# Sending eighteen more transposes of a decoder kernel through DRAM instead of through TensorE

## The chip, the core and the metric

The kernel runs on one core of one Trainium2 chip. The metric is the device time of one launch in microseconds (us), the median of several runs. Five engines work side by side, each through its own list of instructions in order: PE (TensorE: matmuls and the transposes that are made as matmuls; PEld is its weight load), DVE (VectorE), ACT (ScalarE), POOL (GpSimd) and SP (SyncE), which here issues every DMA. An instruction that has to wait holds up everything behind it on its engine.

## What is computed

Two blocks, one behind the other, on x of 256 rows by 1024. Where the change works:

```python
for l in range(2):                                     # first block
    proj = x @ w_in[l]                                 # split into cb,cc,ch,dq,dk,dv,iq,ik,iw,cq,ck,cv
    y = concat(conv(cb,cc,ch), dsa_attention(dq,dk,dv,iq,ik,iw), chunk_band_attention(cq,ck,cv))
    x = layer_norm(ALPHA*x + y @ w_mix_out[l])
    q = x @ w_mq[l]; k, v = split(mem @ w_mkv[l])      # memory cross attention, 4 heads of 256
    x = layer_norm(ALPHA*x + softmax(q k' / 16) v @ w_mo[l])
    x = layer_norm(ALPHA*x + squared_relu(x @ w_ff1[l]) @ w_ff2[l])
for i in range(4):                                     # second block
    mix = retention | dilated attention | gMLP | retention
    # gMLP: s = tril(w_s[g]) @ vn + b_s,  mix = (u * s) @ w_out
    x = x + rmsnorm(mix); x = x + rmsnorm(swiglu(rmsnorm(x))); x = x + gate * (p[i] @ w_proj)
```

Every projection is made in split precision: a 32-bit operand is cut into a high part and the rest, and three matmuls (high x high, high x rest, rest x high) are added.

## The kernel before

The 256 rows are two tiles of 128, each worked by its own generator, "thread 0" and "thread 1". Both use one stream of weight blocks, so a block is loaded and cut once; thread 1 follows thread 0 by a few blocks. A block is 512 KB (384 KB for the groups named cq, ck and cv): `load` issues its DMA on SP into one of 5 raw buffers, `split` has ACT cast the high part `wh` (L284 or L225) and DVE subtract the rest `wl` (L232 or L228); the raw buffer is free again when the rest has been cut, and so DVE sets when SP may issue the load five blocks on.

`proj` (L402) makes one 512-wide projection from four blocks and calls `flush` behind each block; `flush` runs work that was put off to that place: `due` counts down in blocks, `behind` holds the attention heads of a mixer, one step a block. The order of the instructions on each engine is then set by a scheduler, which works with its own estimates of durations; it places the DMA issues in SP's list too.

Matmuls need their left operand transposed. There are two ways to get it:

- `transpose4` (L276): up to four 128x128 matmuls by an identity (L279) into one PSUM bank, then one copy out of the bank by ACT or DVE. The tiles are called cqp, ckp, mTp, mqp and wsp at the five places of this change.
- `trip` (L356) and what calls it: DVE transposes 32x32 blocks into `xt` (L360), four DMAs write it to a DRAM tile `xd` (L364), and one DMA reads it back in turned order (L376, L380 or L386). `turn_to` then copies it in place with ACT (L377), `turn_by_dma` cuts it into high part and rest (L397, L398). The read is put off by BACK = 1 block, the copy by CUT = 3 blocks. `xt` shares two buffers with `ET`, the turned softmax weights of all attention heads, over both threads.

In a mixer (`mixer`, L625) the groups come in the order A, B, cq, ck, cv, F, H, then the memory keys and values (mkv), then the output projection. A and B end in an index score of which DVE takes the 64 largest entries of each row in 8 rounds of MAX8 and MATCH_REPLACE (L689, L690) while PE works on cq and ck. The heads of the first attention (`six_heads` on dqT and dkT: scores `sp`, softmax `ss`, transposes `ptp`, product with the values) run beside cv and F, those of the chunk attention (on cqT and ckT) beside H and mkv. In the first layer the 256 memory rows are transposed too (`memory_rows`, L619), once for both layers.

Of the kernel before, what the change touches and what calls it, by code (L numbers as in the profile page):

```python
# [15 lines left out]
P = 128  # L16
# [14 lines left out]
DEFER = (1, 1, 1, 1, 1, 1, 1, 1)  # L31
# [17 lines left out]
def kernel(  # L49
# [226 lines left out]
    def transpose4(t, srcs, nm, kind="tr"):  # L276
        p = bank(kind, t, [P, 4, P], nm)
        for i, s in enumerate(srcs):
            T.transpose(p[:, i, :], s, ident)  # L279
        return p  # L280
# [26 lines left out]
    def newbank(t):  # L307
        return tuple(sb.tile([P, 4, P], F32R, tag=f"h{t}", name=f"part{t}", bufs=8) for _ in range(2))

    def cut(bank, sl, src, scale=1.0, rows=slice(0, P), hi_eng="s"):  # L310

        hi, lo = bank[0][rows, sl, :], bank[1][rows, sl, :]
        if scale == 1.0:
            copy(hi_eng, hi, src)
            V.tensor_tensor(out=lo, in0=src, in1=hi.bitcast(F32), op=ALU.subtract)
        else:
            S.activation(hi, src, AF.Copy, scale=scale)
            V.scalar_tensor_tensor(out=lo, in0=src, scalar=scale, in1=hi.bitcast(F32), op0=ALU.mult,
                                   op1=ALU.subtract)
# [29 lines left out]
    def defer(t, on, fn):  # L349
        if on:  # L350
            later[t].append(fn)
        else:
            fn()
# [28 lines left out]
    def turn_by_dma(t, src, nkk, parts, j, square=None, at=CUT):  # L382

        back = trip(t, src, nkk)
        z = src
        put_off(t, BACK, lambda: nc.sync.dma_start(z, back))  # L386

        def fin():
            bank = parts.banks[j] = newbank(t)
            zv = z.rearrange("p (i k b) -> p k i b", i=4, k=nkk)  # L390
            hi, lo = (x[:, 0:nkk, :].rearrange("p k (i b) -> p k i b", i=4) for x in bank)
            if square:
                f = sb.tile([P, 4, P], F32, tag=f"tq{t}", name="ffT", bufs=2)
                S.activation(f[:, 0:nkk, :].rearrange("p k (i b) -> p k i b", i=4), zv, AF.Square, scale=square)
                cut(bank, slice(0, nkk), f[:, 0:nkk, :])
            else:
                S.copy(hi, zv)  # L397
                V.tensor_tensor(out=lo, in0=zv, in1=hi.bitcast(F32), op=ALU.subtract)  # L398

        put_off(t, at, fin)  # L400
# [218 lines left out]
    def memory_rows(t):  # L619
        rows = tiles[("memr", t)]  # L620
        m_ = Parts()
        mh = sb.tile([P, 8, P], F32R, tag=f"x{t}", name=f"memHi{t}")
        for b in range(2):
            p = transpose4(t, [rows[:, (4 * b + i) * P:(4 * b + i + 1) * P] for i in range(4)], "mTp")
            m_.banks.append((mh[:, 4 * b:4 * b + 4, :], memLo[:, t, 4 * b:4 * b + 4, :]))  # L625
            cut(m_.banks[b], slice(0, 4), p)
        memT[t] = m_


    def mixer(t, l, xT):  # L630
# [118 lines left out]
        S.copy(cq[:, :384], pq[:, :384])  # L749
        cqT = sb.tile([P, 3, P], F32, tag=f"tq{t}", name="cqT", bufs=2)  # L750

        def turn(src, dst, nm):
            p = transpose4(t, [src[:, i * P:(i + 1) * P] for i in range(3)], nm)
            S.copy(dst, p[:, 0:3, :])

        defer(t, DEFER[6], lambda: turn(cq, cqT, "cqp"))
        if l == 0:
            defer(t, DEFER[6], lambda: memory_rows(t))
        pk = yield from proj(t, xT, ("ck", l), 384)
        ck = sb.tile([P, 512], F32, tag=f"rB{t}", name="ck", bufs=2)  # L760
        S.copy(ck[:, :384], pk[:, :384])
        ckT = get2(("ckT", l), [P, 3, 256], "kv", 4)
        defer(t, DEFER[6], lambda: turn(ck, ckT[:, :, own], "ckp"))

        behind[t].append(six_heads(dqT, lambda h, r: dkT[r:r + 64, :nk], lambda kt, h: shared[("dv", l, kt)],
                                   lambda hs: score.rearrange("p (o k) -> p o k", o=1).to_broadcast([P, len(hs), nk]),
# [73 lines left out]
    def cross(t, l, xT):  # L840
        qT = []
        oT = Parts()
        for j in range(2):
            p = yield from proj(t, xT, ("mq", l, j), 512)
            q = sb.tile([P, 512], F32, tag=f"rA{t}", name="mqr", bufs=2)
            if j:
                V.tensor_scalar(out=q, in0=p, scalar1=0.0625, scalar2=None, op0=ALU.mult)
            else:
                S.mul(q, p, 0.0625)
            pt = transpose4(t, [q[:, i * P:(i + 1) * P] for i in range(4)], "mqp")  # L850
            qT.append(sb.tile([P, 4, P], F32, tag=f"tq{t}", name="mqT", bufs=2))
            copy("s" if j else "v", qT[j], pt)
        for b in range(2):
            kT = shared[("mkT", l, b)]
            sp = bank("at", t, [P, 2, 256], "msp")
            for i in range(2):
                for c in range(2):
                    T.matmul(sp[:, i, :].rearrange("p (i b) -> p i b", b=32), qT[b][:, 2 * i + c, :], kT[:, :, 2 * i + c, :],
                             start=(c == 0), stop=(c == 1))
            pt, et, ev = turn_bank(t, softmax_bank(t, sp, 2, 2), 2)  # L860
            copy("v", et, pt)
            o = pt
            for i in range(2):
                for c in range(2):
                    c0 = 512 * b + 256 * i + 128 * c
                    for kt in range(2):
                        T.matmul(o[:, 2 * i + c, :], shared[("mv", l, kt)][:, c0:c0 + P], ev[:, i, kt, :],
                                 start=(kt == 0), stop=(kt == 1))
            oT.banks.append(newbank(t))
            cut(oT.banks[b], slice(0, 4), o, IALPHA)  # L870
        acc = newacc(t)
        yield from outproj(t, acc, ("mo", l), 8, oT, 0, True, True, xT)
        return acc
# [194 lines left out]
    def gmlp(t, hT, rs):  # L1068
        if t == 0:
            ws = tiles[("gws",)]  # L1070
            G.affine_select(out=ws, in_=ws, pattern=[[0, 8], [-1, P]], compare_op=ALU.is_ge, fill=0.0, base=0,
                            channel_multiplier=1)
            wsT = sb.tile([P, 8, P], F32, tag="kv", name="wsT", bufs=4)
            for b in range(2):
                pt = transpose4(t, [ws[:, 4 * b + k, :] for k in range(4)], "wsp")
                V.tensor_copy(wsT[:, 4 * b:4 * b + 4, :], pt)
            shared["wsT"] = wsT
        wsT = shared["wsT"]
        st_ = small([P, 4, 6], f"gst{t}")
        vs = []  # L1080
        for j in range(4):
            p = yield from proj(t, hT, ("gv", j), 512)
            tag, nb = (f"U{t}", 3) if j < 3 else (EB[0].format(t=t), EB[1])
            v = sb.tile([P, 512], F32, tag=tag, name="gvr", bufs=nb)
            S.activation(v, p, AF.Gelu, scale=rs[:, 0:1])
            V.bn_stats(out=st_[:, j, :], in_=v)
            vs.append(v)
        mv = small([P, 2], f"mv{t}")
        V.bn_aggr(out=mv, in_=st_)
        ve = small([P, 1], f"ve{t}")  # L1090
        V.tensor_scalar(out=ve, in0=mv[:, 1:2], scalar1=EPS, scalar2=None, op0=ALU.add)
        r2 = small([P, 1], f"rs{t}")
        rsqrt(r2, ve)
        gg, gb = tiles[("gmg",)], tiles[("gmb",)]
        for j in range(4):
            sl = slice(512 * j, 512 * j + 512)
            V.tensor_scalar(out=vs[j], in0=vs[j], scalar1=mv[:, 0:1], scalar2=r2[:, 0:1],  # L1097
                            op0=ALU.subtract, op1=ALU.mult)
            V.tensor_tensor(out=vs[j], in0=vs[j], in1=gg[:, sl], op=ALU.mult)  # L1099
            (V if j == 0 else G).tensor_tensor(out=vs[j], in0=vs[j], in1=gb[:, sl], op=ALU.add)  # L1100
        acc = newacc(t)
        oT = Parts()
        for j in range(5):
            if j < 4:
                p = yield from proj(t, hT, ("gu", j), 512)
                u = sb.tile([P, 512], F32, tag=f"rA{t}", name="gur", bufs=2)
                S.activation(u, p, AF.Gelu, scale=rs[:, 0:1])
                sp = bank("tr", t, [P, 2, 256], "gsp")
                o = sb.tile([P, 512], F32, tag=f"rB{t}", name="gor", bufs=2)
                for k in range(2):  # L1110
                    g = 2 * j + k
                    T.matmul(sp[:, k, :], wsT[:, g, :], vs[j][:, 256 * k:256 * k + 256], start=True, stop=True)  # L1112
                for k in range(2):
                    g = 2 * j + k
                    V.scalar_tensor_tensor(out=o[:, 256 * k:256 * k + 256], in0=sp[:, k, :], scalar=gbs[:, g:g + 1],
                                           in1=u[:, 256 * k:256 * k + 256], op0=ALU.add, op1=ALU.mult)
                oT.banks.append(None)
                turn_by_dma(t, o, 4, oT, j)
            if j > 0:
                yield from outproj(t, acc, ("go", j - 1), 4, oT, 4 * j - 4, j == 1, j == 4)  # L1120
        return acc
# [213 lines left out]
```

## Time and profile before

| | |
|---|---|
| median of 3 runs | 2572.3 us (2567.38 to 2573.31) |
| profiled execution | 2566.06 us, its span 2564.3 us, granted TensorE clock 0.999 |
| PE busy | 2521.9 us, 98% of the span |
| DVE / ACT busy | 1823.3 us (71%) / 1501.9 us (59%) |
| DMA engines | 66.4% busy for the queue that SP feeds, 205 GB/s of HBM traffic over the span |

Times in the rows below count from the start of the span. A busy time holds the whole length of each instruction; matmuls are pipelined, so two starts can lie closer together than one of them is long. In brackets at the end of a timeline row stand the idle time of the engine before it and what ended that.

### The profile page before, as it was taken

To read this page: it belongs to the slowest core of one execution; us is meant where nothing else is said; L and a number is where in the kernel's file an instruction comes from. 1 tells how busy PE (TensorE), PEld (TensorE's weight loads), DVE (VectorE), ACT (ScalarE), POOL (GpSimd) and SP (SyncE) were. 2 spreads that over 40 slices of the span, in tenths; PEclk is the share of its full clock that TensorE was granted. 3 is DMA by queue.
4 is the path that set the end of the run, shared out by engine and by line. 5 is a ranking of instruction groups with operands and counts; after the bars stand their busy time and mean duration, and the time that the engine had idled before them with its cause. 6 is when DMAs were issued, how large, how long until landed. Compare 5 with 4: busy or idle time off the path is not lost. (4 is left out here: it accounts for less than half of the span.)

```text
span 2564.3 us, 36170 instructions
## 1 busy us (share of the span) xinstructions
PE 2521.9 (98%) x12100; PEld 2059.6 (80%) x12100; DVE 1823.3 (71%) x3357; ACT 1501.9 (59%) x2856; POOL 60.0 (2%) x88
## 2 busy tenths in 40 slices
PE   8999999999999999999999999999999999999999
PEld 7787787887788778788777787888877887887887
DVE  8865767866766876766866767767767678766666
ACT  6653555654455565555766666557656557565555
POOL 0000000000000000000000000000100000000000
PEclk9999999999999999999999999999999999999999
DMA  6463776554578677677766665777576776766774
GB/s 214 150 215 103 224 245 187 171 192 156 155 233 244 190 235 248 190 240 219 221 204 209 194 208 179 230 214 223 170 257 212 226 221 196 255 220 193 230 208 159
DMA packets 321227, 528.27 MB, mean 206 GB/s; under 512 B 37392, under 2 KB 135824, under 8 KB 319888
## 3 DMA queue, kind: packets, MB, share of 16 engines
q1 hardware_dynamic: 321040, 525.96, 66.4%
q8 instruction: 95, 1.56, 0.3%
q14 instruction: 92, 0.75, 0.1%
HBM read 484.96 MB, written 40.89 MB: 205 GB/s over the span
## 5 line engine op out<-in xcount | busy, mean ns | idle before, releaser
L326 PE MATMUL pj<-wh,part 128*128 128x512 f32 (+3 forms) x4480 | 1415.4, 384 | 4.9 <-ACT part L284 1.4
L326 PEld LDWEIGHTS pj<-wh,part 128*128 128x128 f32 x4480 | 831.2, 188 | 174.3 <-issue 8.9
L326 PE MATMUL pj<-wl,part 128*128 128x512 f32 (+3 forms) x2240 | 852.9, 381 | 1.3 <-DVE wl L228 1.3
L326 PE MATMUL acc<-wh,part 128*128 128x512 f32 x1920 | 582.2, 395 | 12.8 <-ACT part L284 5.9
L326 PEld LDWEIGHTS pj<-wl,part 128*128 128x128 f32 x2240 | 421.9, 188 | 79.1 <-DVE wl L228 2.7
L326 PEld LDWEIGHTS acc<-wh,part 128*128 128x128 f32 x1920 | 356.8, 189 | 92.5 <-ACT part L284 8.4
L326 PE MATMUL acc<-wl,part 128*128 128x512 f32 x960 | 307.1, 393 | 0.1
L232 DVE TENSOR_TENSOR wl<-ff,wh 128x512 fp32r<-128x512 f32 x256 | 169.6, 686 | 102.9 <-ACT wh L284 102.6
L284 ACT CAST wh<-ff 128x512 fp32r<-128x512 f32 x256 | 152.4, 620 | 131.5 <-PE acc L326 64.6
L326 PEld LDWEIGHTS acc<-wl,part 128*128 128x128 f32 x960 | 180.8, 188 | 38.3 <-DVE wl L232 0.6
L225 ACT ACTIVATE wh<-fg,ngc 128x512 fp32r<-128x512 f32 (+1 forms) x192 | 126.5, 686 | 116.3 <-PE pj L326 60.7
L228 DVE SCALAR_TENSOR_TENSOR wl<-fg,ngc,wh 128x512 fp32r<-128x512 f32 (+1 forms) x192 | 129.5, 702 | 74.2 <-ACT wh L225 74.1
L228 DVE SCALAR_TENSOR_TENSOR wl<-fu,ngc,wh 128x512 fp32r<-128x512 f32 (+1 forms) x192 | 128.1, 704 | 53.8 <-ACT wh L225 47.9
L225 ACT ACTIVATE wh<-fu,ngc 128x512 fp32r<-128x512 f32 (+1 forms) x192 | 123.5, 684 | 62.2 <-PE acc L326 38.5
L284 ACT CAST wh<-fo 128x512 fp32r<-128x512 f32 x176 | 103.7, 621 | 76.9 <-PE pj L326 72.4
L232 DVE TENSOR_TENSOR wl<-fo,wh 128x512 fp32r<-128x512 f32 x176 | 114.9, 685 | 42.2 <-ACT wh L284 39.5
L232 DVE TENSOR_TENSOR wl<-mkv,wh 128x512 fp32r<-128x512 f32 x64 | 41.9, 687 | 27.0 <-ACT wh L284 26.9
L228 DVE SCALAR_TENSOR_TENSOR wl<-rg,ngc,wh 128x512 fp32r<-128x512 f32 x64 | 44.9, 748 | 19.7 <-ACT wh L225 19.6
L284 ACT CAST wh<-mkv 128x512 fp32r<-128x512 f32 x64 | 37.5, 620 | 36.2 <-PE acc L326 21.2
L228 DVE SCALAR_TENSOR_TENSOR wl<-pg,ngc,wh 128x512 fp32r<-128x512 f32 x64 | 46.3, 748 | 15.9 <-ACT wh L225 15.4
L225 ACT ACTIVATE wh<-rv,ngc 128x512 fp32r<-128x512 f32 x64 | 43.2, 718 | 21.6 <-PE pj L326 9.3
L232 DVE TENSOR_TENSOR wl<-ro,wh 128x512 fp32r<-128x512 f32 x64 | 42.8, 686 | 18.1 <-ACT wh L284 18.0
(315 smaller groups left out, 3175.8 us busy)
## 6 DMA issues: line engine op xcount, KB each, us to landing
ff<-in_w_ff_dram SPq DMA_DIRECT2D x128, 512.0 KB, 4.4
fo<-in_ffn_out_dram SPq DMA_DIRECT2D x88, 512.0 KB, 4.4
fg<-in_ffn_in_dram SPq DMA_DIRECT2D x80, 512.0 KB, 4.5
fu<-in_ffn_in_dram SPq DMA_DIRECT2D x80, 512.0 KB, 4.3
xd<-xt SPq DMA_DIRECT2D x576, 64.0 KB, 2.4
mkv<-in_w_mkv_dram SPq DMA_DIRECT2D x32, 512.0 KB, 4.6
rv<-in_ret_in_dram SPq DMA_DIRECT2D x32, 512.0 KB, 5.5
rg<-in_ret_in_dram SPq DMA_DIRECT2D x32, 512.0 KB, 4.2
```

What stands on the lines that cost most here:

```text
L225: S.activation(h_, r_, AF.Copy, scale=gc)
L228: V.scalar_tensor_tensor(out=l_, in0=r_, scalar=gc, in1=h_.bitcast(F32), op0=ALU.mult, op1=ALU.subtract)
L232: (V if le == "v" else G).tensor_tensor(out=l_, in0=r_, in1=h_.bitcast(F32), op=ALU.subtract)
L284: S.copy(o, i)
L326: T.matmul(outs[i], a, ws[i][b], start=s0, stop=s1)
```

## The change

```diff
--- before.py
+++ after.py
@@ -386,7 +386,7 @@
         put_off(t, BACK, lambda: nc.sync.dma_start(z, back))
 
         def fin():
-            bank = parts.banks[j] = newbank(t)
+            bank = parts.banks[j] = parts.banks[j] or newbank(t)
             zv = z.rearrange("p (i k b) -> p k i b", i=4, k=nkk)
             hi, lo = (x[:, 0:nkk, :].rearrange("p k (i b) -> p k i b", i=4) for x in bank)
             if square:
@@ -621,9 +621,8 @@
         m_ = Parts()
         mh = sb.tile([P, 8, P], F32R, tag=f"x{t}", name=f"memHi{t}")
         for b in range(2):
-            p = transpose4(t, [rows[:, (4 * b + i) * P:(4 * b + i + 1) * P] for i in range(4)], "mTp")
             m_.banks.append((mh[:, 4 * b:4 * b + 4, :], memLo[:, t, 4 * b:4 * b + 4, :]))
-            cut(m_.banks[b], slice(0, 4), p)
+            turn_by_dma(t, rows[:, 512 * b:512 * b + 512], 4, m_, b, at=4 + 2 * b)
         memT[t] = m_
 
 
@@ -749,18 +748,14 @@
         S.copy(cq[:, :384], pq[:, :384])
         cqT = sb.tile([P, 3, P], F32, tag=f"tq{t}", name="cqT", bufs=2)
 
-        def turn(src, dst, nm):
-            p = transpose4(t, [src[:, i * P:(i + 1) * P] for i in range(3)], nm)
-            S.copy(dst, p[:, 0:3, :])
-
-        defer(t, DEFER[6], lambda: turn(cq, cqT, "cqp"))
+        turn_to(t, cq[:, :384], 3, cqT)
         if l == 0:
             defer(t, DEFER[6], lambda: memory_rows(t))
         pk = yield from proj(t, xT, ("ck", l), 384)
         ck = sb.tile([P, 512], F32, tag=f"rB{t}", name="ck", bufs=2)
         S.copy(ck[:, :384], pk[:, :384])
         ckT = get2(("ckT", l), [P, 3, 256], "kv", 4)
-        defer(t, DEFER[6], lambda: turn(ck, ckT[:, :, own], "ckp"))
+        turn_to(t, ck[:, :384], 3, ckT[:, :, own])
 
         behind[t].append(six_heads(dqT, lambda h, r: dkT[r:r + 64, :nk], lambda kt, h: shared[("dv", l, kt)],
                                    lambda hs: score.rearrange("p (o k) -> p o k", o=1).to_broadcast([P, len(hs), nk]),
@@ -847,9 +842,12 @@
                 V.tensor_scalar(out=q, in0=p, scalar1=0.0625, scalar2=None, op0=ALU.mult)
             else:
                 S.mul(q, p, 0.0625)
-            pt = transpose4(t, [q[:, i * P:(i + 1) * P] for i in range(4)], "mqp")
             qT.append(sb.tile([P, 4, P], F32, tag=f"tq{t}", name="mqT", bufs=2))
-            copy("s" if j else "v", qT[j], pt)
+            if j:
+                pt = transpose4(t, [q[:, i * P:(i + 1) * P] for i in range(4)], "mqp")
+                S.copy(qT[j], pt)
+            else:
+                turn_to(t, q, 4, qT[j])
         for b in range(2):
             kT = shared[("mkT", l, b)]
             sp = bank("at", t, [P, 2, 256], "msp")
@@ -1072,8 +1070,7 @@
                             channel_multiplier=1)
             wsT = sb.tile([P, 8, P], F32, tag="kv", name="wsT", bufs=4)
             for b in range(2):
-                pt = transpose4(t, [ws[:, 4 * b + k, :] for k in range(4)], "wsp")
-                V.tensor_copy(wsT[:, 4 * b:4 * b + 4, :], pt)
+                turn_to(t, ws[:, 4 * b:4 * b + 4, :].rearrange("p g m -> p (g m)"), 4, wsT[:, 4 * b:4 * b + 4, :])
             shared["wsT"] = wsT
         wsT = shared["wsT"]
         st_ = small([P, 4, 6], f"gst{t}")
```

At five places a trip takes the place of transposes on PE and of the copy out of PSUM: cq and ck (each layer and thread, three 128x128 each), the first half of the memory queries mq (each layer and thread, four each), the memory rows (each thread, two halves of four, first layer alone; the cut comes 4 and 6 blocks on) and the gMLP weights (two halves of four, thread 0 alone). That is 64 transposes in 18 groups; each group becomes one DVE block transpose, four DMAs out, one DMA back and one copy or cut. The change at L389 lets `turn_by_dma` write into a bank that is there already.

The order moves in the first mixer, in the second mixer, at the two cross attentions and at the start of the gMLP, and nowhere else. SP in the first mixer, before, from the third cv block on (cv, F and H are weight groups; the index behind the name is the block):

```order
L199 DMA cv_2_673<-in_w_in_dram 128x2x384
L199 DMA cv_3_719<-in_w_in_dram 128x2x384
L199 DMA F_0_761<-in_w_in_dram 128x2x512
L199 DMA F_1_783<-in_w_in_dram 128x2x512
L199 DMA F_2_809<-in_w_in_dram 128x2x512
L199 DMA F_3_873<-in_w_in_dram 128x2x512
```

The same place of SP with the change (memr_242 and memr_244 are the memory rows of thread 0 and 1; 32x4x96 is a quarter of a cq or ck trip, 32x4x128 of a memory trip):

```order
L199 DMA cv_2_680<-in_w_in_dram 128x2x384
L364 DMA xd<-xt 32x4x128 x8
L376 DMA cq<-xd 128x384
L386 DMA memr_242<-xd 128x512
L364 DMA xd<-xt 32x4x96
L386 DMA memr_242<-xd 128x512
L364 DMA xd<-xt 32x4x96 x3
L199 DMA cv_3_731<-in_w_in_dram 128x2x384
L364 DMA xd<-xt 32x4x128 x8
L376 DMA cq<-xd 128x384
L386 DMA memr_244<-xd 128x512
L199 DMA F_0_771<-in_w_in_dram 128x2x512
```

Between the loads of cv_2 and F_0, where one load stood, there are now that load and 24 other DMAs, eight of them the two halves of thread 1's memory rows.

DVE in the first mixer, before, at the softmax of thread 1's first four heads (ss is the softmax tile, rcs the reciprocal of its sums, wl the rest of a weight block):

```order
L710 TENSOR_REDUCE nmx_931<-ss 128x2
L318 SCALAR_TENSOR_TENSOR part_125<-ptp,part_124 64x384 x2
L716 RECIPROCAL rcs_925<-sume_922 128x2
L232 TENSOR_TENSOR wl<-F_2_809,wh 128x512
L718 TENSOR_SCALAR ss<-ss,rcs_925 128x256 x2
L716 RECIPROCAL rcs_936<-sume_933 128x2
L232 TENSOR_TENSOR wl<-F_3_873,wh 128x512
L718 TENSOR_SCALAR ss<-ss,rcs_936 128x256 x2
```

The same softmax on DVE with the change:

```order
L709 TENSOR_REDUCE nmx_955<-ss 128x2
L715 RECIPROCAL rcs_949<-sume_946 128x2
L717 TENSOR_SCALAR ss<-ss,rcs_949 128x256 x2
L715 RECIPROCAL rcs_960<-sume_957 128x2
L717 TENSOR_SCALAR ss<-ss,rcs_960 128x256
L360 STREAM_TRANSPOSE xt<-memr_244 128x512
L717 TENSOR_SCALAR ss<-ss,rcs_960 128x256
L232 TENSOR_TENSOR wl<-cv_3_731,wh 128x384 x2
L360 STREAM_TRANSPOSE xt<-ck 128x384 x2
L398 TENSOR_TENSOR memLo<-memr_244,memHi_753 128x512
L232 TENSOR_TENSOR wl<-F_0_771,wh 128x512 x2
```

Before, the cuts of F stood ahead of this softmax and in it; now the second half of thread 1's memory rows is transposed in it, and the cuts of cv_3 and of F_0 come behind it.

SP in the second mixer with the change (before, the loads cv_3, F_0 to F_3 follow each other there without a trip between them):

```order
L199 DMA cv_3_5292<-in_w_in_dram 128x2x384
L199 DMA F_0_5315<-in_w_in_dram 128x2x512
L364 DMA xd<-xt 32x4x96 x6
L376 DMA cq<-xd 128x384
L364 DMA xd<-xt 32x4x96 x2
L199 DMA F_1_5338<-in_w_in_dram 128x2x512
```

Here F_0 is loaded ahead of all trips, and the first trip behind it.

## Rows read from the trace of the kernel before

**Rows 1.** The page's first part: busy time, share and instructions of each engine.

```profile
PE 2521.9 (98%) x12100; PEld 2059.6 (80%) x12100; DVE 1823.3 (71%) x3357; ACT 1501.9 (59%) x2856; POOL 60.0 (2%) x88
```

**Rows 2.** Busy time in stretches: PE, PEld, DVE, ACT, POOL, clock, DMA share, GB/s.

```profile
40.00:60.00 20.00, 18.29 (x116) 16.58 (x115) 19.55 (x58) 11.38 (x26) 0.14 (x1) 1.00 0.52 141
60.00:80.00 20.00, 18.65 (x115) 14.97 (x114) 16.36 (x42) 14.80 (x42) 0.00 (x0) 1.00 0.43 135
480.00:500.00 20.00, 19.11 (x123) 17.15 (x122) 19.07 (x53) 12.38 (x32) 0.00 (x0) 1.00 0.54 158
```

**Rows 3.** Timeline of PE in the first mixer: start, length, instruction, count.

```profile
45.02 0.49 PE L279 MATMUL cqp<-tab,cq 128*128 128x128 f32 x3
45.34 0.60 PE L279 MATMUL mTp<-tab,memr 128*128 128x128 f32 x4
45.70 0.42 PE L326 MATMUL pj<-wh,part 128*128 128x384 f32 x1
46.95 0.66 PE L279 MATMUL mTp<-tab,memr 128*128 128x128 f32 x4 [0.83 <-ACT cqT L754]
...
50.39 0.44 PE L326 MATMUL pj<-wh,part 128*128 128x384 f32 x1 [0.87 <-ACT cq L749]
```

**Rows 4.** The tile mTp: durations in ns (least/median/most), first and last start.

```profile
L279 PE MATMUL mTp<-tab,memr x16: 272/273/329, 45.3 to 53.0; 128*128 128x128 f32 x16
...
L315 DVE TENSOR_TENSOR memLo<-mTp,memHi x4: 681/687/693, 47.4 to 54.1; 128x512 fp32r<-128x512 f32 x4
```

**Rows 5.** The tile xt: the block transposes of the trips that are there.

```profile
L360 DVE STREAM_TRANSPOSE xt<-mk x8: 701/710/712, 115.6 to 552.6; 128x512 f32<-128x512 f32 x8
L360 DVE STREAM_TRANSPOSE xt<-pr x8: 437/439/442, 1158.9 to 2464.2; 128x256 f32<-128x256 f32 x8
```

**Rows 6.** DMA issues by line: count, KB each, median us to landing.

```profile
xd<-xt SPq DMA_DIRECT2D x576, 64.0 KB, 2.4
```

**Rows 7.** Timeline of SP in the first mixer.

```profile
51.62 6.89 SPq L199 DMA_DIRECT2D F<-in_w_in_dram  x4
...
116.32 1.78 SPq L364 DMA_DIRECT2D xd<-xt  x4
```

**Rows 8.** The tile F in the first mixer: ACT's cast, and issue to landing of its loads.

```profile
L284 ACT CAST wh<-F x8: 617/620/624, 56.6 to 67.4; 128x512 fp32r<-128x512 f32 x8
...
DMA to landing us min/median/max: 3.6/4.3/4.8
```

**Rows 9.** Timeline of DVE in the first mixer: end of the score, then two softmaxes.

```profile
56.39 0.29 DVE L691 TENSOR_SCALAR score<-score 128x256 f32<-128x256 f32 x1
...
59.54 1.02 DVE L707 SCALAR_TENSOR_TENSOR ss<-sp,score 128x384 f32<-128x384 f32 x2
60.48 1.00 DVE L710 TENSOR_REDUCE nmx<-ss 128x3 f32<-128x384 f32 x2
...
69.15 1.27 DVE L710 TENSOR_REDUCE nmx<-ss 128x2 f32<-128x512 f32 x2
```

**Rows 10.** Timeline of ACT there: the first softmax and its table load.

```profile
62.34 1.28 ACT L713 ACT_TABLE_LOAD   x1
63.63 0.40 ACT L713 ACTIVATE ss<-ss,nmx 128x128 f32<-128x128 f32 x1
...
71.25 0.51 ACT L713 ACTIVATE ss<-ss,nmx 128x256 f32<-128x256 f32 x1
```

**Rows 11.** Timeline of PE there: cv, thread 0's softmax, the first block of F.

```profile
59.89 0.51 PE L326 MATMUL pj<-wh,part 128*128 128x384 f32 x2
...
60.41 0.51 PE L326 MATMUL pj<-wh,part 128*128 128x384 f32 x2
...
65.57 0.30 PE L279 MATMUL ptp<-tab,ss 128*128 128x128 f32 x1 [1.35 <-DVE ss L718]
...
69.51 0.87 PE L735 MATMUL ptp<-ET,dv 128*64 128x128 f32 x6
...
74.25 0.48 PE L326 MATMUL pj<-wh,part 128*128 128x512 f32 x1
```

## The prediction

> **What bounds the kernel now.** I read the page's first part first: PE is busy 2521.9 of the span's 2564.3 us [rows 1], so the 42 us of PE's idle time and the length of its list are all that there is to gain. Then the stretches in which the change works [rows 2]: the clock stands at 1.00 of the 2.4 GHz level and does not enter the sum. What does is that the two mixers are the places where a second engine is full as well: DVE is busy 19.55 of 20 us at 40 to 60 and 19.07 of 20 at 480 to 500, and PE lacks 1.71, 1.35 and 0.89 us in the three stretches. Then, for the first mixer, the timelines of PE, SP, DVE and ACT [rows 3, 7, 9 to 11]. The reader is to see there how far ahead of their use weights are loaded: F's loads are issued at 51.62 to 58.5, its first matmul runs at 74.25. That lead, some 22 us, is what the change spends.
>
> The sum is made against the profiled execution, 2566.06 us (the span and 1.8 us around it); the median of the runs shown is 2572.3, 6.2 us above it. I put the difference on the median.
>
> **What goes.** 64 transposes in 18 groups. What one costs PE is the gap between starts, not its length: the three of cqp hold PE from 45.02 to 45.34, 0.32 us, the four of mTp from 45.34 to 45.70, 0.36 us [rows 3]. Eight groups of three (cqp, ckp) by 0.32 is 2.6 us, ten groups of four (mTp 4, mqp 4, wsp 2) by 0.36 is 3.6 us: 6.2 us of PE time. With them go two waits in the first mixer, 0.83 us of the second mTp group for its bank (ACT was still copying cqp) and 0.87 us at 50.39, where ACT was late with cq's evacuation since it had memory rows to cut [rows 3]. One mTp transpose is 273 ns long [rows 4], and that is not what PE gets back.
>
> By the Trainium skill, in TensorE: Matmul & The Clock Gate, Part 4, a transpose on PE takes about 275 ns in a kernel's context; the trace has 273 ns for the length and so agrees, but a sum by that figure is the second rival below, since four starts here lie within 0.36 us.
>
> **What comes.** Each group becomes a DVE block transpose (0.71 us for 512 columns; 0.44 for 256, so 0.57 for 384) [rows 5], four DMAs out (SP is busy 1.78 us with them [rows 7], and they land 2.4 us after issue [rows 6]), one read back, and the copy or cut, now from SBUF. ACT copies cq and ck as before, it gets six copies more (mq, gMLP); where they fall it is not the bound. DVE gets 4 x 0.71 for the memory rows and 8 x 0.57 for cq and ck, 7.4 us; at mq and the gMLP the block transpose stands in for a PSUM copy of about the same length. The reads wait for the writes, and behind them on SP wait the weight loads: that is the added wait that counts.
>
> *Second mixer.* Four groups of three go, -1.3 us. F_0 is loaded there ahead of all trips (the order shows it), so no load is late. DVE is full, and four block transposes of 0.57 push the first softmax: +0.5 (PE waits for such a softmax at 65.57 for 1.35 us in the first mixer [rows 11], and will be there sooner). Net -0.8, bounds -1.3 to +2 (2.3 us of DVE, nearly all coming through).
>
> *Cross attentions.* Four groups of four go, -1.4. The turned queries are needed only after the whole second mq block, and the scores that use them come in the new order behind four further matmuls of thread 1. I add 0.5 for the later start of thread 0's softmax: -0.9, bounds -1.4 to +2.
>
> *gMLP.* Two groups, -0.7. The scheduler hoists these trips ahead, they depend on no activation, and the weights are used a projection group later. Bounds -0.7 to +1.
>
> *First mixer.* Here the change is worked out as a chain. Before, the index score ends at 56.68 [rows 9]. Ahead of it DVE loses the four memory rests (0.69 each [rows 4]), which move behind it, and gets three block transposes (0.57 + 2 x 0.71): it ends at 55.9. Then thread 0's softmax: add 1.0, reductions 1.0 with thread 1's cq transpose (0.57) between [rows 9]; ACT, from the first reduction at 57.4, its table load 1.28 and six exponentials of 0.40 [rows 10], so 61.1; DVE's scaling, 62. Thread 1: two adds and two memory rests at 0.69, two reductions 1.27 [rows 9], so 66; two exponentials of 0.5 [rows 10], 67; reciprocal and scaling 0.5 and, in the middle of it, the block transpose of the second half of thread 1's memory rows, 0.71. That ends at X = 68.
>
> From X two chains run. PE has the last two softmax transposes and the twelve matmuls of cv_3 (0.173 us each by 59.89 and 60.41 [rows 11]), 2.6 us, and then wants F_0. SP has four writes (1.78), two reads (0.9 at the same rate) and then F_0's load: landed 4.3 us later, cast in 0.62 [rows 8], so X + 7.6. Whatever X is, PE waits 5 us. F's first matmul runs at 75.6 against 74.25: +1.4, although PE has saved 2.7 us of transposes and the two waits of 1.7 by then. At that moment it has less behind it: the six value products of thread 0, which stood at 69.51 and in pairs before it [rows 11], are still to come (1.5 us; four softmax transposes, 0.4, are done earlier): +1.1. F_1 stands behind the read that waits for thread 1's last writes, F_2 and F_3 behind the writes and reads of ck, and the copies into ET behind ck's xt buffers: together +2.5 by the same rates, between 0 and 6. The mixer ends 5.0 later. Bounds: -4.4, if no load comes late (2.7 + 1.7), to +11, if the slowest landing of a load (4.8 [rows 8]) and a wait of half of F_0's at each of F_1 to F_3 come on top. I take 5.0, since the order of DVE and SP leaves F_0 no other place.
>
> Sum: 5.0 - 0.8 - 0.9 - 0.7 = +2.6 us: 2568.7 for the profiled execution, 2575 on the median. Ends: -7.8 (2564.5) and +16 (2588).
>
> **Rivals.**
> 1. *All trips are hidden.* For it: the lead of 22 us, and DMA engines that are at 0.52 and 0.43 in the first mixer [rows 2]. Against it: F_0 behind 24 DMAs on SP. It gives 6.2 + 1.7 less, 2564.5.
> 2. *Each transpose gives back its length.* 64 x 0.273 is 17.5 us, 2555. Against it: the starts [rows 3].
> 3. *SP becomes the bound of the first mixer* (slower). The eight trips share two xt buffers with ET; a block transpose on DVE waits until the four writes of the trip two before have landed (1.78 + 2.4 us and what SP waits for in between), and the cuts behind it on DVE, which free the raw buffers, wait too. If SP turns so from one late load to a row of them, each of F_0 to F_3 costs PE what F_0 does: 4 x 5 less 4.4, +16, 2588. It decides from the point at which X comes later than 73, for then the lead of H and mkv is gone as well. For it: 19.55 of 20 us of DVE [rows 2]; against it: a DMA share of half.
>
> By the Trainium skill, in VectorE: DVE Perf Modes, Rules for kernel authors, a 128x128 transpose belongs on TensorE where PSUM is a fit destination, as it was here. By that rule the change loses at every place and rival 3 is the likelier; the full DVE of the first mixer agrees with it, the free DVE of the gMLP does not.
>
> **How the numbers follow.** Forecast 0.62 (its own range 2568 to 2581), rival 1 0.12, rival 2 0.02, rival 3 0.24. About 0.3%, 7.7 us, can be told from no change here. Rival 1 reaches that just so, with rival 2 faster has 0.12; slower has rival 3's 0.24 and a little of the forecast's upper edge, 0.25; the same 0.63. The range runs from rival 1 to rival 3, 2564 to 2588.
>
> **What would show it.** Right: PE idle in front of the first F matmul for about 5 us, released by a cast that waited for F_0's DMA; F_0's issue near 71 instead of 51.62; PE idle at 60 to 80 of 6 us or more against 1.35; no new idle at 180 to 200 and 1780 to 1800. Wrong: F_0 issued before 62, then rival 1; casts waiting for DMA at F_1 to F_3 and H too, then rival 3; a step where PE waits at msp or gsp for a turned tile, then my three small terms.

## The result and the profile after

The changed kernel took 2583.31 us in the median (2578.54 to 2590.56, 6 executions) against 2568.68 beside it: a ratio of 1.0058, 95% interval 1.0042 to 1.0073. It is slower, by 14.6 us, more than the 0.3% that can be told from no change. That lies inside the stated range (2564 to 2588), and outside the forecast's own range of 2568 to 2581: the forecast had been 2575 and "the same", a change of +2.6 us on the 2572.3 of three runs.

Where the time went can be read from one instruction that both kernels have. The transposes of `z` on PE (xTp) stand behind the normalisations of the two layers, the first of them right behind the first mixer. First the tile xTp in the trace of before, then in that of after (durations in ns, first and last start, shape):

```profile
L572 PE MATMUL xTp<-tab,z x80: 270/272/331, 165.4 to 681.8; 128*128 128x128 f32 x80
```

```profile
L572 PE MATMUL xTp<-tab,z x80: 270/272/330, 176.9 to 692.9; 128*128 128x128 f32 x80
```

The first mixer ends 11.5 us later; at the last of these rows, two cross attentions and a second mixer further on, it is 11.1. So of what is lost in the two layers, nearly all is lost in the first 177 us. In the second block the transposes of `x` stand behind its normalisations, again before and after:

```profile
L279 PE MATMUL xTp<-tab,x x192: 270/272/331, 854.6 to 2537.6; 128*128 128x128 f32 x192
```

```profile
L279 PE MATMUL xTp<-tab,x x192: 270/273/421, 865.0 to 2554.6; 128*128 128x128 f32 x192
```

At the first of them the difference is 10.4 us, at the last 17.0, at the end of the spans 17.2. What comes on top here lies in the second block, where the change touches the gMLP alone. From its first row to the end of the span the block takes 1709.7 us in the trace of before, the least of all, and 1711.7 to 1719.5 in the twelve profiles of the table below, whose kernels have the same instructions there. So these traces don't tell how much of it the change makes. The first mixer makes two thirds of the difference between the two traces; the part in the second block is open.

Stretches of [rows 2], after:

```profile
40.00:60.00 20.00, 19.92 (x117) 17.50 (x115) 19.50 (x61) 8.57 (x21) 0.14 (x1) 1.00 0.50 123
60.00:80.00 20.00, 12.07 (x52) 9.67 (x51) 13.34 (x32) 10.77 (x30) 0.00 (x0) 0.78 0.66 193
...
480.00:500.00 20.00, 19.31 (x115) 17.61 (x115) 19.76 (x75) 12.46 (x25) 0.29 (x2) 1.00 0.41 102
```

At 40 to 60 PE is fuller than before: the waits of 0.83 and 0.87 us are gone, with the transposes. At 60 to 80 it is busy 12.07 us against 18.65, and the granted clock, 1.00 before, is 0.78. DVE is not the fuller for it there: 13.34 against 16.36.

SP's timeline after, from cv_3's load on (it answers to [rows 7]):

```profile
60.83 0.40 SPq L199 DMA_DIRECT2D cv<-in_w_in_dram  x1
61.46 8.93 SPq L364 DMA_DIRECT2D xd<-xt  x8
70.49 0.39 SPq L376 DMA_DIRECT2D cq<-xd  x1
70.99 0.39 SPq L386 DMA_DIRECT2D memr<-xd  x1
71.43 0.43 SPq L199 DMA_DIRECT2D F<-in_w_in_dram  x1
72.02 0.34 SPq L386 DMA_DIRECT2D memr<-xd  x1
72.41 0.43 SPq L199 DMA_DIRECT2D F<-in_w_in_dram  x1
72.88 2.30 SPq L364 DMA_DIRECT2D xd<-xt  x4
75.28 0.44 SPq L199 DMA_DIRECT2D F<-in_w_in_dram  x1
```

Eight writes take SP 8.93 us, of which issuing is some 3.6 (1.78 for four [rows 7]): it stood in the middle of them until DVE had transposed the second half of thread 1's memory rows. F_0's load, issued at 51.62 before, is issued at 71.43. DVE's timeline at that place (to [rows 9]):

```profile
67.61 0.35 DVE L717 TENSOR_SCALAR ss<-ss,rcs 128x256 f32<-128x256 f32 x1
67.87 0.70 DVE L360 STREAM_TRANSPOSE xt<-memr 128x512 f32<-128x512 f32 x1
68.50 0.31 DVE L717 TENSOR_SCALAR ss<-ss,rcs 128x256 f32<-128x256 f32 x1
```

And PE's, with its waits (to [rows 11]):

```profile
66.79 0.63 PE L279 MATMUL ptp<-tab,ss 128*128 128x128 f32 x4 [1.61 <-DVE ss L717]
68.11 1.46 PE L279 MATMUL ptp<-tab,ss 128*128 128x128 f32 x4 [0.69 <-DVE ss L717]
...
77.08 0.79 PE L326 MATMUL pj<-wh,part 128*128 128x512 f32 x1 [4.61 <-ACT wh L284]
...
86.39 0.87 PE L734 MATMUL ptp<-ET,dv 128*64 128x128 f32 x6 [0.57 <-ACT ET L284]
88.11 1.09 PE L734 MATMUL ptp<-ET,dv 128*64 128x128 f32 x8 [0.85 <-DVE ET L286]
```

PE stands 4.61 us before F's first matmul, and 2.3 us at two softmax tiles ahead of that. In the bracket stands ACT's cast, but ACT had been waiting itself, for the DMA: its own row, from ACT's timeline after, says so:

```profile
76.41 1.14 ACT L284 CAST wh<-F 128x512 fp32r<-128x512 f32 x2 [1.62 <-DMA F<-in_w_in_dram]
```

Summed over PE's timeline, its waits between 40 us and the first of the xTp rows are 12.18 us after and 3.58 before: 8.6 more, of which the 2.7 us of transposes saved take back a part. The other 5.6 of the 11.5 us are not waits that the trace names. They lie in PE's busy time: from 40 us to the first xTp row it is 124.46 us after and 121.63 before, although 2.7 us of transposes are gone. The low clock between 68 and 81 is the candidate, and was tried below.

### The profile page after: what moved, and what is told of

It is laid out like the page before. It is cut to its first block, busy times and chain, and to the rows that moved or that the text cites. A ratio compares the mean times of both kernels' runs of the same rounds, so it can differ in the third digit from the quotient of the medians.

```text
span 2581.5 us, 36215 instructions
## 1 busy us (share of the span) xinstructions
PE 2525.9 (98%) x12036; PEld 2059.5 (80%) x12036; DVE 1829.7 (71%) x3369; ACT 1503.3 (58%) x2862; POOL 59.8 (2%) x88
```

## The experiments

All against the kernel before, on the chip beside it. "Clock" is the mean of the granted clock over the executions of a kernel (before: 0.9984 over 29, and 0.9982 over 25 and 0.9978 over 20 beside the later kernels); "mixer" is the first start of xTp from z in the profiled execution, 165.4 before. That is one execution of each: the slowest of its kernel for mem_pe and memonly, the fastest for cqck0_pe. L0 and L1 are the two layers.

| kernel | trips that stay, and what else | median us | ratio (95%) | clock | mixer |
|---|---|---|---|---|---|
| the change | all | 2583.3 | 1.0058 (1.0042 to 1.0073) | 0.9953 | 176.9 |
| mqws | mq, gMLP | 2566.6 | 0.9991 (0.9982 to 0.9999) | 0.9982 | 164.9 |
| mix0_pe | mq, gMLP, cq/ck of L1 | 2570.0 | 1.0005 (0.9996 to 1.0014) | 0.9978 | 165.6 |
| mem_pe | all but memory | 2573.3 | 1.0017 (1.0003 to 1.0030) | 0.9973 | 171.5 |
| cqck0_pe | all but cq/ck of L0 | 2575.5 | 1.0026 (1.0015 to 1.0036) | 0.9965 | 165.5 |
| cqck0_again | the same | 2576.8 | 1.0026 (1.0013 to 1.0038) | 0.9970 | 167.6 |
| memonly | mq, gMLP, memory | 2569.1 | 1.0003 (0.9992 to 1.0013) | 0.9980 | 166.0 |
| mem_late | all, memory behind F | 2575.0 | 1.0024 (1.0011 to 1.0037) | 0.9976 | 167.5 |
| poolq | all, first mixer's on POOL | 2578.9 | 1.0037 (1.0024 to 1.0049) | 0.9968 | 166.7 |
| l1pe | all but cq/ck of L1 | 2582.9 | 1.0053 (1.0035 to 1.0070) | 0.9952 | 177.5 |
| poolq_l1pe | as l1pe, first mixer's on POOL | 2569.0 | 1.0005 (0.9996 to 1.0015) | 0.9978 | 166.2 |
| fill | all, fillers on PE | 2582.0 | 1.0053 (1.0041 to 1.0065) | 0.9967 | 178.1 |

**Which part of the change.** Four kernels undo parts of it: first both parts of the first mixer, then the memory rows alone, then cq and ck of the first layer alone, and at last all of cq, ck and memory. The edits put the lines of before back, under a condition:

```diff
-        turn_to(t, cq[:, :384], 3, cqT)
+        if l == 0:       # mix0_pe, cqck0_pe; always in mqws
+            defer(t, DEFER[6], lambda: turn(cq, cqT, "cqp"))
+        else:
+            turn_to(t, cq[:, :384], 3, cqT)      # and ck likewise
-            turn_by_dma(t, rows[:, 512 * b:512 * b + 512], 4, m_, b, at=4 + 2 * b)
+            p = transpose4(...)                  # mix0_pe, mem_pe, mqws
+            cut(m_.banks[b], slice(0, 4), p)
```

> The changed kernel with the first layer's cq, ck and memory rows turned on PE again; the trips of the second layer's cq and ck, of both layers' mq and of the gMLP weights stay. Theory Q (the loss sits in the first mixer: on SP F_0's load stands behind the trips, PE waits 4.6 us for it and runs at a lower clock around that): the first mixer is that of before, the rest gives what the trace of after shows from the first mixer's end to the end of the second layer (from +11.5 to +10.4, so -1.1) and at the gMLP (-1.3): 2566, 2564 to 2568. Rival D (the +6 us that the trace of after gathers in the second block belongs to the change): 2572 to 2575.

> The changed kernel with the memory rows alone turned on PE again. In SP's order F_0's load then stands behind thread 1's cq writes and the load of cv_3, ahead of every ck trip. Theory Q: F_0 is issued near 61 instead of 71.4, no wait for a load, no lower clock; first mixer within 1 us of before: 2567, 2565 to 2570. Rival V (DVE: the block transposes that stand in the softmax chain make PE wait for softmax tiles, 0.9 + 1.6 + 0.7 us by 61 to 68, and lower the clock): four of the seven block transposes there stay, so about half of the 11.5 us stays: 2573, 2571 to 2576.

> The changed kernel with the first layer's cq and ck turned on PE again; the memory rows' trips stay. F_0's load stands behind thread 1's eight memory writes and one read, F_1 behind the other read, F_2 and F_3 behind nothing. Theory Q: F_0 is issued near 68 to 70 and PE waits 3 to 4 us for it; F_1 to F_3 follow at once: 2576, 2573 to 2580. Rival V: the loss follows the block transposes, of which four of 0.71 stay and four of 0.57 go, so somewhat over half stays: 2575. By itself it does not part the two; with the run before it does: Q wants nearly all of the loss here and none there, V half and half.

> Only the trips of mq (both layers) and of the gMLP weights; cq, ck and the memory rows are turned on PE everywhere. PE loses six groups of four, 2.1 us by the gaps between starts. Theory A (beside those places other work covers the trips): 2566.5, 2565 to 2568, mean granted clock that of before (0.998). Rival B (PE's saved time comes back as waits, as the cross attentions of the changed kernel's trace suggest, which gained 0.2 to 0.5 us instead of 1.4): 2568 to 2570.

With both parts of the first mixer on PE the loss is gone as far as can be told (mix0_pe, 1.0005); its 2570.0 lies between what theory Q and rival D wanted. mqws, which keeps the gMLP's trips, is faster than before, 0.9991, by 0.3 to 4.6 us, where 2.1 were expected of six groups of four: the gMLP's trips, the only ones in the second block, cost nothing that shows, and rival D falls. Neither of the first mixer's two parts makes the whole: memory rows alone or cq and ck alone add 0.21 or 0.12% to mix0_pe's ratio, both together 0.53%.

As times, the pair of mem_pe and cqck0_pe came out as rival V had it (2573 and 2575); theory Q had 2567 for mem_pe and missed it. In the execution of mem_pe that was profiled, its slowest, the first mixer ends 6.1 us later than before, where Q wanted it within 1: no load is late there, but PE waits 1.70 us at cq, 1.49 at cf and 1.10 at mk. The pair does not decide for V: both kernels have the second layer's trips too, which have a price of their own (below), the memory rows' four block transposes without these cost no more than can be told (memonly, 1.0003), and the queue is tried further on. What the pair does show stands in SP's list. Either part alone leaves F_0 early: issued at 55.97 with the memory rows alone, at 56.66 with cq and ck alone. My expectation for cqck0_pe, 68 to 70, missed: without cq's and ck's trips the transposes of the memory rows come early, the third and fourth here (cqck0_pe, DVE, where after has them at 60.73 and 67.87):

```profile
49.71 0.70 DVE L360 STREAM_TRANSPOSE xt<-memr 128x512 f32<-128x512 f32 x1
50.69 0.70 DVE L360 STREAM_TRANSPOSE xt<-memr 128x512 f32<-128x512 f32 x1
```

So it is the eight trips together that push the last transposes into the softmax, and F_0 with them. In the changed kernel DVE does not stand idle in front of either transpose, so their place in its list made them late; whether the two shared buffers are the reason for that place was not tried.

**The queue.** The trips' DMAs go through POOL's queue instead of SP's, DVE's work stays.

```diff
-            nc.sync.dma_start(dv[:, :, i, :].rearrange(...), ...)
+            DQ_[0].dma_start(dv[:, :, i, :].rearrange(...), ...)   # the reads likewise
-        turn_to(t, cq[:, :384], 3, cqT)
+        on_queue(nc.gpsimd if l == 0 else nc.sync, turn_to, t, cq[:, :384], 3, cqT)  # ck, memory likewise
```

> The changed kernel with the DMAs of the first layer's cq, ck and memory trips issued by POOL (its queue is nearly empty there) instead of SP; the order of DVE changes little, its work not at all. The weight loads then stand one behind another on SP as before. Theory Q: F_0 is issued before 62, PE does not wait for it: 2567, 2564 to 2571 (the upper end if POOL's DMAs are slow and ckT is late). Rival V: DVE has the same block transposes in the softmax chain, so 2577 to 2583. Rival R (the raw buffers: DVE cuts late, so the loads are late whatever queue they stand in): F_0 is issued after 66 here too, 2577 or more.

The first mixer is cured (166.7, F_0 issued at 51.61), the time is not: 1.0037, and 2578.9 lies where rivals V and R had it. The trace put most of the rest into the second mixer, whose trips are on SP still and whose order had changed. So the pair was made again without the second layer's cq and ck:

> The kernel with the first layer's trips on POOL's queue, with cq and ck of the second layer turned on PE. In the trace with POOL's queue the first mixer ended 1.3 us later than before and the second one 6.5 us later still; there the order of the second mixer had changed too. Theory Q: the first mixer keeps +1.3, the second is that of before, mq and gMLP as in the other kernels: 2569, 2566 to 2572. Rival P (trips by POOL are dear in themselves, in the time of the DMAs and by what runs beside them, so that lower clock and small waits stay): 2575 to 2579.

> The changed kernel with cq and ck of the second layer turned on PE; the first mixer's eight trips on SP, in the order of the changed kernel. It differs from the kernel of 2569.0 us (the first layer's trips on POOL's queue) in the queue of those trips and in what the scheduler makes of it. Theory Q (SP's queue): the first mixer of the changed kernel's trace, +11.5 at its end, -2.1 for mq and gMLP: 2578, 2575 to 2581, mean clock 0.996. Rival S (most of the changed kernel's loss sits in the second mixer and in what the clock does there): 2571 to 2574, for the kernel with the trips on POOL and the second layer's on SP came to 2578.9.

This is the pair that decides: 2582.9 with the eight trips on SP, 2569.0 with them on POOL. SP's timeline in poolq_l1pe has nothing but loads,

```profile
44.65 5.45 SPq L199 DMA_DIRECT2D cv<-in_w_in_dram  x3
51.39 8.07 SPq L199 DMA_DIRECT2D F<-in_w_in_dram  x4
61.04 12.68 SPq L199 DMA_DIRECT2D H<-in_w_in_dram  x4
```

and DVE transposes the last half of the memory rows as late as in the changed kernel:

```profile
67.99 0.70 DVE L367 STREAM_TRANSPOSE xt<-memr 128x512 f32<-128x512 f32 x1
```

The block transposes on DVE (rival V) are thereby out as the main cause: all of them are there in poolq_l1pe. So are late raw buffers (rival R): the same loads go out from 51.39 us on, as before the change. In l1pe the wait before F is that of the changed kernel and longer (PE's timeline of l1pe):

```profile
77.98 0.79 PE L326 MATMUL pj<-wh,part 128*128 128x512 f32 x1 [6.23 <-ACT wh L284]
```

The scheduler orders the two kernels somewhat differently (DVE's list too), so the 13.9 us are the queue and what the scheduler makes of it. Rival S (the second mixer) falls with the 2582.9 of l1pe, which passes theory Q's upper end of 2581 as well. On POOL's queue the eight trips bring no gain either: 1.0005, against 0.9991 for mqws, which turns the same tiles on PE.

**The memory rows at another place.**

```diff
-        if l == 0:
-            defer(t, DEFER[6], lambda: memory_rows(t))
...
         pF = yield from proj(t, xT, ("F", l), 512)
+        if l == 0:
+            memory_rows(t)                        # with at=3 + b
```

> The changed kernel with the memory rows' trips issued behind F instead of behind cq (their cut one or two blocks after the read). DVE, SP and xt do the same work, at another place: on SP F_0's load stands behind one cq trip, the memory trips stand among the loads of mkv. Theory Q (what costs is that F's loads stand behind the trips in one queue): the first mixer is that of the kernel with the memory rows on PE, 2573, 2570 to 2576, mean clock near 0.997. Rival V (the amount of work for DVE, SP and the two xt buffers in the mixer): 2580 or more, clock 0.995 to 0.996. Rival M (mkv's loads come late instead): PE waits for a cast at mkv_0_2 or mkv_0_3, 2576 to 2580.

2575.0 and a first mixer of 167.5: the amount of work stayed, its place changed, and over half of the loss went (1.0024 against 1.0058). The waits that rival M wanted are small (0.62 us at a cast at 110.2, 1.29 at a copy into ET at 108.0). What is left, as in poolq, lies behind the first mixer.

**The clock.** Fillers on PE in the wait before F_0; SP's order is the same word for word.

```diff
         S.copy(cv, pv[:, :384])
+        if l == 0 and t == 1:
+            for _ in range(6):
+                transpose4(t, [cv[:, (i % 3) * P:(i % 3 + 1) * P] for i in range(4)], "fil")
```

> The changed kernel with 24 transposes on PE whose result nobody reads, between the last matmul of cv_3 for thread 1 and the first of F_0, where PE waited 4.6 us; SP's order is the same word for word. At the full clock they take 2.4 us and lie within that wait. Theory C (half of the 14.6 us that the change costs is the clock, which falls after PE has stood still; the mean granted clock of the changed kernel's runs is 0.9953 against 0.9984): the clock stays up at 75 to 81, 2 to 3 us less, 2580 to 2581.5, mean clock 0.996 to 0.997. Rival W (the clock has fallen at 68 already, by the softmax waits of 61 to 68, and the fillers at the low clock take 4.8 us): F_0 starts at the same time or up to 1 us later, 2583 to 2584.5, mean clock 0.995.

In the changed kernel, at 57 to 72, 72 to 80 and 80 to 92 us (PE, PEld, DVE, ACT, POOL, clock, DMA share, GB/s):

```profile
57.00:72.00 15.00, 11.69 (x63) 9.77 (x62) 11.95 (x32) 8.93 (x28) 0.00 (x0) 0.89 0.50 127
72.00:80.00 8.00, 3.39 (x9) 2.24 (x8) 3.89 (x7) 4.50 (x9) 0.00 (x0) 0.66 0.97 313
80.00:92.00 12.00, 10.58 (x56) 7.87 (x56) 4.54 (x9) 4.13 (x9) 0.00 (x0) 0.94 0.54 159
```

and with the fillers:

```profile
57.00:72.00 15.00, 11.70 (x63) 9.78 (x62) 12.48 (x32) 8.63 (x27) 0.00 (x0) 0.89 0.52 131
72.00:80.00 8.00, 5.79 (x37) 4.50 (x35) 3.17 (x5) 3.73 (x7) 0.00 (x0) 1.00 0.96 305
80.00:92.00 12.00, 9.65 (x54) 6.90 (x53) 5.18 (x9) 4.89 (x10) 0.00 (x0) 1.00 0.54 164
```

The clock stays up, as theory C wanted, and the mixer ends no sooner (178.1). F_0's load is issued at 72.09 there, 0.7 us later than in the changed kernel; from that issue to the end of the mixer it is 106.0 us, against 105.5. F's matmuls now run fast and wait for the next load instead (PE's timeline of fill):

```profile
73.75 2.84 PE L279 MATMUL fil<-tab,cv 128*128 128x128 f32 x24 [0.57 <-ACT cv L765]
78.01 0.51 PE L326 MATMUL pj<-wh,part 128*128 128x512 f32 x1 [1.42 <-ACT wh L284]
...
80.86 0.49 PE L326 MATMUL pj<-wh,part 128*128 128x512 f32 x1 [0.69 <-ACT wh L284]
```

So in these two executions the low clock at 72 to 81 cost nothing; the loads set the pace there. The fall of the clock at 68 to 72, behind the softmax waits, is in both, and its price stays open. By the medians the kernel gained 1.4 us, with intervals that lie over each other, between the two expectations: the times decide nothing here, the trace does.

**What is left behind the first mixer.**

> The trips of the memory rows, mq and the gMLP weights; cq and ck turned on PE in both layers. With the second layer's cq and ck going by the trip this kernel had 2575.5 us in the median, although the first mixer of its profiled execution ended where that of before does (F_0's load was issued at 55.97) and that execution took 2569.2. Theory Q: F_0's load is early, so the memory rows are hidden and the second mixer carries what was lost: 2567, 2565 to 2570. Rival X (the memory rows' trips cost about 5 us in most executions, by something that the one profile did not show): 2571 to 2575, the mean clock near 0.997.

> The kernel with the first layer's cq and ck on PE once more, for a second profiled execution beside the first, which was the fastest of its 12. Theory Q: an execution of 2574 or more shows its loss after the first mixer (in the second mixer, or at stretches of lower clock), and the first mixer ends within 1 us of before's 165.4. Rival X: the first mixer ends 3 us or more later, with F_0 or a memory cut late.

memonly, 2569.1, is cqck0_pe without the second layer's cq and ck: 0.23% apart, so theory Q holds there and X does not. For cqck0_again neither holds: Q wanted the first mixer to end within 1 us of before, X at least 3 us later with a load or a cut late, and it ended 2.2 us later with F_0 issued at 55.86. The second profile of cqck0_pe is of a slower execution (the profile's span is 2579.9 us, 2567.1 in the first), and the second layer's mixer ends 429.4 us behind the first (before 419.7, first profile 419.0). What the same program adds in the slower execution are waits, the first and the third of them followed by a granted clock of 0.50, the 1.2 GHz level (PE's timeline of cqck0_again):

```profile
422.31 1.22 PE L326 MATMUL acc<-wh,part 128*128 128x512 f32 x2 [3.41 <-ACT part L284]
...
532.41 0.39 PE L326 MATMUL pj<-wh,part 128*128 128x256 f32 x1 [1.12 <-ACT cf L783]
535.33 0.30 PE L279 MATMUL ptp<-tab,ss 128*128 128x128 f32 x1 [1.32 <-DVE ss L717]
```

The first stands in the feed forward, which the change does not touch; memonly, in its slowest execution, has a wait of 3.90 us at the same matmul, without a trip in the second mixer. The other two stand in the second mixer, where poolq and mem_late have a softmax wait of 1.29 too.

## Why the prediction was right and wrong

*PE's gain by the gaps between starts* (2.1 us for the six groups of mq and gMLP): right within the interval, mqws measured 0.9991, some 2.3 us (0.3 to 4.6). Rival 2, the full length of each transpose, would have been 6.5 us for these 24.

*The chain to F_0*: right, nearly to the microsecond. Predicted: the second half of thread 1's memory rows transposed at X = 68, F_0 issued near 71, PE waiting 5 us, F's first matmul at 75.6. Measured: 68.5, 71.43, 4.61, 77.08; PE idle at 60 to 80 came to 7.93 us, where 6 or more was the sign. The start of F is late since F's loads took 5.0 us to land (median, 40 to 100 us) against the 4.3 of [rows 8], with DMA engines busy 0.97 of 72 to 80.

*What follows F_0*: the step that failed. "Together +2.5 by the same rates", and 1.1 for the value products, was taken for what is lost between F's first matmul and the end of the mixer; it was 8.7 (11.5 less 2.8). PE's waits from 80 us to there came to 4.35 against 0.53: three for ET's copies, the softmaxes of the second half, a copy of mk. Those 3.8 us more are not the whole of 8.7; what the rest is stays open. The bound, +11 for the mixer, had it almost; the value did not. The mechanism up to F_0 was right; what follows it was put at 3.6 us and measured 8.7, well over twice that.

*"The clock ... does not enter the sum"*: wrong as read from the trace of before, since a wait that the change makes can bring it down: 0.78 at 60 to 80. But its price at 72 to 81 is nothing by fill, so what it adds to the tail is not settled.

*Second mixer*, -0.8: wrong in sign. The second layer's cq and ck cost 0.14% (mix0_pe against mqws), 0.23% (cqck0_pe against memonly), 0.32% (poolq against poolq_l1pe) and 0.05% (the change against l1pe). The upper bound, +2 or 0.08%, is passed in three of the four, and in the second and third the two intervals lie apart. The traces say the same. From the end of the first layer to the end of the second mixer, by the first xTp row behind each, it takes 153.8 us before and 161.1 in poolq:

```profile
431.35 0.33 PE L572 MATMUL xTp<-tab,z 128*128 128x128 f32 x1 [0.27 <-DVE z L568]
585.15 0.33 PE L572 MATMUL xTp<-tab,z 128*128 128x128 f32 x1 [0.36 <-DVE z L568]
```

```profile
431.73 0.33 PE L581 MATMUL xTp<-tab,z 128*128 128x128 f32 x1 [0.24 <-DVE z L577]
592.86 0.33 PE L581 MATMUL xTp<-tab,z 128*128 128x128 f32 x1 [0.36 <-DVE z L577]
```

The five profiles of kernels without these trips have 153.3 to 153.9 us for this stretch, the eight of kernels with them 154.2 to 161.1, that of the change 154.6. F_0 is early there, as forecast; the waits are at softmax tiles and at cf, in some executions and not in others, and why is open.

*Cross attentions and gMLP*: right in sum, as far as mqws can tell. From the first to the second normalisation the traces have 79.1 and 79.2 us in the two layers before and 78.7 and 78.8 after, 0.8 us together for the -0.9 forecast.

*Rivals.* Rival 1 had "all hidden": mqws is what of the change is hidden. Rival 3, SP as the bound from X = 73 on, gave 2588; X stayed at 68.5, yet 2583 lies nearer to it than to 2575: SP's queue cost more than the one load that I let it delay. By the Trainium skill (VectorE: DVE Perf Modes, Rules for kernel authors) a 128x128 transpose belongs on TensorE where PSUM will do. The runs agree for the first mixer, where the trips lose on SP and gain nothing on POOL's queue, and disagree, if only just, for mq and gMLP (0.9991). The size of the loss is the queue's: l1pe and poolq_l1pe have the same work on DVE.

## What to carry to other kernels

Before transposes go over DRAM, look at what stands behind their DMAs in the queue that issues them: here eight trips cost 14 us more in the queue of the weight loads than in one that was nearly empty. Two edits that each leave a load early can together make it late, so such edits are tried together. Count a late load with what it shifts behind it, not with the wait in front of it alone: the wait was 4.6 us, the loss 11.5.

## What the runs showed of the hardware

The granted clock differs between executions of one program, and with it the time. mem_pe took 2566.56 us at a mean clock of 0.999 and 2580.45 at 0.995; over the 29 executions of before the time falls by 2.3 us per 0.001 of clock (least squares; 1.5 over the set of 25 and 2.8 over that of 20; 0.001 of the span is 2.6 us). In the slowest execution of mem_pe PE stood 1.49 us at 95.1, and the clock was 0.50 (1.2 GHz) in the windows from 96 to 102, while in before's profile a wait of 1.35 us [rows 11] was followed by none. A profile is one draw of this: of cqck0_pe one ended the second mixer at 584.5 us and the other at 597.0. The changed kernel's clock, 0.9953 on the mean against 0.9984, would be some 8 us if each 0.001 cost that much; fill shows a stretch in which it did not.
